# Products in two parts for the experts' units of 128 slots, results added with exact ones, and weights in ten tiles of 1 MB

## The chip, the cores and the metric

The kernel runs on one core of one Trainium2 chip. The time is device microseconds of one execution of the whole program; each number below says whether it is a median of runs or the execution that was profiled. Engines: PE is TensorE (products), PEld its loading of the stationary operand, DVE VectorE, ACT ScalarE, POOL GpSimd; SP issues DMA transfers. A bank is one of the eight accumulators of TensorE, 128 rows by 512 columns of fp32.

## The reference, cut to what matters

The model has two layers over 256 latent and 256 context tokens of width 1024: an attention layer with a dense feed-forward part, then a state-space layer with a gated linear unit and a mixture of experts. The change lies in the last part alone: eight experts with 3584 hidden columns, each token sent to two of them.

```python
def swiglu(t, w1, w3, w2):
    return (jax.nn.silu(t @ w1) * (t @ w3)) @ w2

def moe_ffn(t, w_router, w1, w3, w2):          # t: 256 x 1024
    logits = (t @ w_router).astype(jnp.float32)
    top_val, top_idx = lax.top_k(logits, TOP_K)          # TOP_K = 2
    gates = jax.nn.softmax(top_val, axis=-1)
    combine = jnp.sum(gates[..., None] * (top_idx[..., None] == jnp.arange(N_EXPERTS)), axis=-2)
    out = jnp.zeros_like(t)
    for e in range(N_EXPERTS):
        out = out + combine[..., e:e + 1] * swiglu(t, w1[e], w3[e], w2[e])
    return out
...
    h = layer_norm(DEEPNORM_ALPHA * h + mod[:, :, 5] * f, ln_g[layer, 1], ln_b[layer, 1])
```

All data are fp32, and the result is wanted to fp32 accuracy.

## The kernel before

Everything ahead of the experts is the same in both kernels. It ends with `n`, two tiles of 128 tokens by 1024, and a table of which token goes to which expert.

**Slots and units.** The experts are ranked by their number of tokens. Rank 0 has room for 192 tokens (slots), the others for 128, 96, 96, 64, 32, 32 and 32 (`CAPS`). What does not fit is left to a loop at the end (`overflow`), which runs no time with these inputs. The slots of an expert are worked on in units of 128, 64 or 32 (`KINDS`): rank 0 has one of 128 and one of 64, rank 1 one of 128, ranks 2 and 3 one of 64 and one of 32, rank 4 one of 64, the last three one of 32. `gather` fills the tile `xg` (1024 x 672 slots, turned) by products of `n` with one-hot matrices `G`.

**Chunks.** The 3584 hidden columns are cut in seven chunks of 512, so there are 56 chunks of 6 MB: a third of `w1` (tile `wa`), one of `w3` (`wb`) and one of `w2` (`wc`), 2 MB each. They pass through a ring of seven tiles (`K.mwb = 7`). The bytes are the same whatever the rank, 336 MB in all; the products are not: ranks 0 to 3 are called heavy, 4 to 7 light. `chunk_order` mixes them by a sum of costs (`COST`): it puts a heavy chunk where the products lag behind the loads, and a light one otherwise. The order that comes out, with H for heavy and L for light, is `LLHLLHLHLLHLLHLLHLLHLHLHLLHLHLHLHLHLHHHLHHHHLHHHHHHHLLLL` and takes the heavy ranks as 0, 1, 2, 3.

**A unit.** `unit_hidden` makes two banks (`p1`, `p3`) in fp32. For 128 slots the weights are the stationary operand, 32 products of 128 columns per matrix (L1517), and the result already lies turned. For 64 or 32 slots the tokens are stationary and the products lie side by side in the columns of the engine (L1526). ACT takes the silu (L1531), DVE multiplies (L1532). `unit_turn` turns a narrow unit's result (L1543), `unit_out` multiplies by `wc` (L1555; 8 products of 512 columns for 128 slots) and adds the two halves to the unit's sum `ya` (L1561, L1563). After the seventh chunk the sum is multiplied by the row `g5` (L1565) and added to both token tiles by `combine` (L1575, L1576), a product with the one-hot matrix of the unit's slots times the gates (`combine_matrix`, L1485, L1487).

**Order.** The loop in `moe` runs one unit ahead: products of `wa` for unit i, the turn of unit i-1, products of `wb` for unit i, `unit_out` of unit i-1. The loads of a chunk are issued on SP's queue when its first unit comes up (L1602, L1605, L1608), each waiting for a free tile. `rest` puts between units the spreading of rows of parameters over partitions (L2147, L2150). `n` and these rows stay in tiles (`rn`, `row`). A scheduler sets the order of the other engines' instructions on their queues from the program order and its own estimates.

Of the kernel before, what the change touches and what calls it, by code (L numbers as in the profile page):

```python
# [20 lines left out]
D = 1024  # L21
# [8 lines left out]
NE = 8  # L30
# [1263 lines left out]
NSLOT = sum(CAPS)  # L1294
ORDER = (7, 0, 6, 1, 2, 5, 3, 4)
# [136 lines left out]
def overflow_list(K, pool, R):  # L1432
# [6 lines left out]
    scr = pool.tile([128, D], F32, tag="ya", name="scr", bufs=4)  # L1439
# [26 lines left out]

def onehots(K, pool, R):
    nc = K.nc
    G = []
    for i in range(2):  # L1470
        G.append(pool.tile([128, NSLOT], F32, tag="ya", name="G", bufs=4))
        for r in range(NE):
            nc.vector.tensor_scalar(G[i][:, BASE[r]:BASE[r] + CAPS[r]], R.iota192[:, :CAPS[r]], R.pos[:, i, r:r + 1], None,
                                    op0=ALU.is_equal)
    return G


def combine_matrix(K, pool, R, kind, base, pos, gate, tag, bufs):
# [7 lines left out]
    c = pool.tile([128, 256], F32, tag=tag, name="cmb", bufs=bufs)  # L1486
# [4 lines left out]
def gather(K, n, G, lo, hi, xg, A, B):  # L1491
    nc = K.nc
    N = hi - lo
    for k in range(8):
# [3 lines left out]
        if k % 2:  # L1498
            nc.scalar.activation(xg[:, k, lo:hi], ps[:, :N], AF.Identity, scale=A[:, k, 1:2], bias=B[:, k, 1:2])
        else:  # L1500
            nc.vector.tensor_scalar(xg[:, k, lo:hi], ps[:, :N], A[:, k, 1:2], B[:, k, 1:2], op0=ALU.mult, op1=ALU.add)


def unit_hidden(K, pool, kind, x, w13a, w13b, between=None):
# [5 lines left out]
    if G == 1:  # L1510
        gT = pool.tile([128, 4, 128], F32, tag="mgT", name="mgT", bufs=4)
        for w, p in ((w13a, p1), (w13b, p3)):
            if between and p is p3:
                between()
            for b in range(4):
                for k in range(8):
                    nc.tensor.matmul(p[:, b * 128:(b + 1) * 128], lhsT=w[:, k, b * 128:(b + 1) * 128],  # L1517
                                     rhs=x[:, k, :], start=(k == 0), stop=(k == 7))
        g = gT.rearrange("p b s -> p (b s)")
    else:  # L1520
        for w, p in ((w13a, p1), (w13b, p3)):
            if between and p is p3:
                between()
            for k in range(8):
                for q in range(G):
                    nc.tensor.matmul(p[kind * q:kind * (q + 1), :N], lhsT=x[:, k, :], rhs=w[:, k, q * N:(q + 1) * N],  # L1526
# [3 lines left out]
    sl = pool.tile([128, 512], F32, tag="msl", name="msl", bufs=2)[:, :N]  # L1530
# [5 lines left out]
def unit_turn(K, pool, kind, st):  # L1536
    gT, g = st
    if gT is None:
        nb = 4 * kind // 128
        gT = pool.tile([128, 4, 128], F32, tag="mgT", name="mgT", bufs=4)  # L1540
# [4 lines left out]
    return gT  # L1545


def unit_out(K, kind, gT, w2, ya, first, last):
# [3 lines left out]
    for b in range(nb):  # L1552
        for hf in range(2):
            for q in range(G):
                K.nc.tensor.matmul(Y[hf][kind * q:kind * (q + 1), :], lhsT=gT[:, b, kind * q:kind * (q + 1)],  # L1555
                                   rhs=w2[:, q * nb + b, hf * 512:(hf + 1) * 512],
                                   start=(b == 0), stop=(b == nb - 1))
    for hf in range(2):
        o = slice(hf * 512, (hf + 1) * 512)
        if first:  # L1560
            K.nc.scalar.copy(ya[:, o], Y[hf])  # L1561
        else:
            K.nc.vector.tensor_tensor(ya[:, o], Y[hf], ya[:, o], op=ALU.add)  # L1563
# [48 lines left out]
def moe(K, pool, R, G, n, A, B, rest):  # L1612
# [19 lines left out]
    def out(j):  # L1632
# [8 lines left out]
        if j["ch"] == final:  # L1641
            combine(K, c, ya.pop(key))
# [631 lines left out]
```

## Time and profile before

| | before |
|---|---|
| median of 3 runs | 1824.44 us (1817.72 to 1825.11) |
| the profiled execution | 1823.15 us |
| its span in the trace | 1821.3 us |
| busy share: PE, PEld, DVE, ACT, POOL | 93%, 64%, 46%, 22%, 11% |
| mean DMA rate over the span | 305 GB/s |
| granted clock of PE, mean | 0.971 of full |

The shares are means over the whole span, of which the experts' stage is the second half; a stage of its own can be quite unlike the mean. A product in fp32 counts as two instructions in the trace. The time of the profiled execution is its span and 1.9 us around it.

### The profile page before, as it was taken

How to read it: one execution, taken by the hardware profiler on the slowest of the kernel's cores; microseconds unless marked ns; L12 is line 12 of the kernel's file. 1: busy time of each engine (PE TensorE's matmuls, PEld its weight loads, DVE VectorE, ACT ScalarE, POOL GpSimd, SP SyncE). 2: the span in 40 equal slices, each digit the busy share in tenths (PEclk: the TensorE clock that was granted, in tenths of full speed). 3: DMA queues.
4: the chain of work that ended last, by engine and by line, in shares of the span. 5: the costliest groups of instructions: out<-in, count | busy, mean ns of one | idle time of the engine just before them, and what ended most of it. 6: DMA issues, size and time to landing. Idle time of an engine off the chain costs nothing.

```text
span 1821.3 us, 34632 instructions
## 1 busy us (share of the span) xinstructions
PE 1687.4 (93%) x14673; PEld 1169.2 (64%) x14673; DVE 835.5 (46%) x1480; ACT 409.5 (22%) x775; POOL 206.1 (11%) x295
## 2 busy tenths in 40 slices
PE   6999997999897999658899999999999999999996
PEld 3755576777675777446577767676667665555553
DVE  2755568858978478995612121113011131241244
ACT  2555543222212355433220000000000001001001
POOL 7910005000000000463120000000000000000000
PEclk9999999999998999788899999999999999999998
DMA  8478752368877776876699799998999998999995
GB/s 318 162 240 270 261 192 82 127 217 278 272 249 239 254 250 202 244 196 264 249 427 401 297 411 389 417 426 350 373 427 412 382 396 322 426 425 377 392 392 207
DMA packets 118391, 556.25 MB, mean 305 GB/s; under 512 B 14616, under 2 KB 47068, under 8 KB 93400
## 3 DMA queue, kind: packets, MB, share of 16 engines
q1 hardware_dynamic: 116800, 550.29, 80.1%
q0 software_dynamic: 1248, 3.10, 0.5%
q8 instruction: 118, 1.93, 0.4%
q10 hardware_dynamic: 184, 0.59, 0.1%
q14 instruction: 41, 0.34, 0.1%
HBM read 529.41 MB, written 24.54 MB: 304 GB/s over the span
## 4 chain that ended last, share of the span: by engine, by line
PE 60%; DVE 10%; DMA 8%; issue 2%; SPq 1%; ACT 1%; POOL 0%; DVEq 0%; ACTq 0%; POOLq 0%
PE bank L1526 18%; PE bank L1555 13%; PE bank L1517 11%; PE bank L57 4%; PE bank L59 4%; PE bank L58 3%; DMA w_d<-wt 2%; PE bank L1575 2%; DMA wraw<-in_ffn_w 1%; PE bank L1497 1%; DMA wb<-in_s_bw 1%; DVE whl L52 1%; PE bank L1543 1%; DVE sG L1122 1%; DMA wa<-in_moe_w 1%
## 5 line engine op out<-in xcount | busy, mean ns | idle before, releaser
L1555 PE MATMUL bank<-wc,mgT 128*32 128x512 f32 (+2 forms) x1200 | 266.0, 598 | 0.5 <-DVE mgT L44 0.5
L1531 ACT ACTIVATE msl<-bank 128x128 f32<-128x128 f32 (+2 forms) x77 | 28.8, 374 | 729.1 <-PE bank L1526 555.3
L52 DVE TENSOR_TENSOR whl<-wraw,whl 128x1024 fp32r<-128x1024 f32 (+3 forms) x126 | 151.0, 1201 | 80.0 <-ACT whl L51 79.9
L59 PE MATMUL bank<-u,whl 128*128 128x512 f32 (+1 forms) x416 | 164.9, 396 | 20.1 <-DVE whl L52 20.1
L51 ACT CAST whl<-wraw 128x1024 fp32r<-128x1024 f32 (+3 forms) x126 | 125.7, 998 | 240.3 <-PE bank L59 109.2
L57 PE MATMUL bank<-u,whl 128*128 128x512 f32 (+1 forms) x416 | 167.4, 402 | 3.9 <-DVE u L52 3.9
L1555 PEld LDWEIGHTS bank<-wc,mgT 128*32 128x32 f32 (+2 forms) x1200 | 85.7, 134 | 132.4 <-issue 127.8
L1526 PE MATMUL bank<-wb,xg 128*32 128x128 f32 (+1 forms) x3136 | 170.5, 304 | 0.0
L1526 PE MATMUL bank<-wa,xg 128*32 128x128 f32 (+1 forms) x3136 | 170.1, 304 | 0.0
L1526 PEld LDWEIGHTS bank<-wa,xg 128*32 128x32 f32 (+1 forms) x3136 | 123.7, 118 | 70.5 <-PE bank L1555 18.7
L58 PE MATMUL bank<-u,whl 128*128 128x512 f32 (+1 forms) x416 | 163.8, 394 | 0.0
L1563 DVE TENSOR_TENSOR ya<-bank,ya 128x512 f32<-128x512 f32 x128 | 88.4, 691 | 139.4 <-PE bank L1555 139.2
L1526 PEld LDWEIGHTS bank<-wb,xg 128*32 128x32 f32 (+1 forms) x3136 | 122.3, 117 | 37.5 <-issue 3.7
L1532 DVE TENSOR_TENSOR msg<-msl,bank 128x128 f32<-128x128 f32 (+1 forms) x63 | 21.9, 347 | 267.7 <-PE bank L1526 267.7
L1517 PEld LDWEIGHTS bank<-xg,wa 128*128 128x128 f32 x896 | 104.4, 196 | 9.9 <-PE bank L1555 6.5
L1517 PE MATMUL bank<-xg,wa 128*128 128x128 f32 x896 | 105.9, 280 | 0.5 <-DMA wa<-in_moe_w 0.5
L59 PEld LDWEIGHTS bank<-u,whl 128*128 128x128 f32 x416 | 80.5, 193 | 40.4 <-DVE whl L52 22.6
L1517 PE MATMUL bank<-xg,wb 128*128 128x128 f32 x896 | 102.3, 275 | 0.0
L1746 POOL TENSOR_TENSOR y<-y,row 128x512 f32<-128x512 f32 x2 | 3.0, 1507 | 875.5 <-ACT y L1745 875.5
L1517 PEld LDWEIGHTS bank<-xg,wb 128*128 128x128 f32 x896 | 101.2, 192 | 0.0
L57 PEld LDWEIGHTS bank<-u,whl 128*128 128x128 f32 x416 | 80.6, 194 | 27.8 <-DVE u L52 4.9
L58 PEld LDWEIGHTS bank<-u,whl 128*128 128x128 f32 x416 | 80.7, 194 | 17.8 <-issue 0.8
(504 smaller groups left out, 2410.1 us busy)
## 6 DMA issues: line engine op xcount, KB each, us to landing
wa<-in_moe_w SPq DMA_DIRECT2D x56, 2048.0 KB
wb<-in_moe_w SPq DMA_DIRECT2D x55, 2048.0 KB
wc<-in_moe_w SPq DMA_DIRECT2D x55, 2048.0 KB
wraw<-in_ffn_w SPq DMA_DIRECT2D x88, 512.0 KB
adaw<-in_ada_w SPq DMA_DIRECT2D x80, 512.0 KB
wraw<-in_w_o SPq DMA_DIRECT2D x16, 512.0 KB
wf<-fs_d SPq DMA_DIRECT2D x32, 256.0 KB
wb<-in_s_bw SPq DMA_DIRECT2D x32, 256.0 KB
```

Source lines behind the costliest of these rows:

```text
L51: K.nc.scalar.copy(hi, src)
L52: (eng or K.nc.vector).tensor_tensor(lo, src, hi.bitcast(F32), op=ALU.subtract)
L57: mm(ps, lhsT=l[0], rhs=r[1], start=start, stop=False)
L58: mm(ps, lhsT=l[0], rhs=r[0], start=False, stop=False)
L59: mm(ps, lhsT=l[1], rhs=r[0], start=False, stop=stop)
L1517: nc.tensor.matmul(p[:, b * 128:(b + 1) * 128], lhsT=w[:, k, b * 128:(b + 1) * 128], rhs=x[:, k, :], start=(k == 0), stop=(k == 7))
L1526: nc.tensor.matmul(p[kind * q:kind * (q + 1), :N], lhsT=x[:, k, :], rhs=w[:, k, q * N:(q + 1) * N], start=(k == 0), stop=(k == 7))
L1531: nc.scalar.activation(sl, p1[:, :N], AF.Silu)
L1532: nc.vector.tensor_tensor(g, sl, p3[:, :N], op=ALU.mult)
L1555: K.nc.tensor.matmul(Y[hf][kind * q:kind * (q + 1), :], lhsT=gT[:, b, kind * q:kind * (q + 1)], rhs=w2[:, q * nb + b, hf * 512:(hf + 1) * ...
L1563: K.nc.vector.tensor_tensor(ya[:, o], Y[hf], ya[:, o], op=ALU.add)
L1575: nc.tensor.matmul(ps, lhsT=c[:, i * 128:(i + 1) * 128], rhs=ya[:, o], start=True, stop=True)
```

## The change

A unit of 128 slots now goes by `wide_hidden`, `wide_turn` and `wide_out`: the tokens are stationary, and each operand is split in a part that is rounded to fp32r (ACT) and the rest of it (DVE, `split`); a product is three passes of 512 columns on the parts (`mm3`). `gather` makes the 256 wide slots in two parts at once. The weights are split when they are needed, in pieces of 128x1024, into pairs of tiles from a ring of four: two of its own, one where `n` lay, one where two parameter rows lay. `Parts.more` makes the splits in program order as far as a pair is free.

The sum of a unit is added with ones: the matrix of slots holds exact ones, the gate is multiplied into the sum on DVE together with `g5`, and the sum is split in two parts (`yh`), so that two passes do. The last expert's sum is added as before.

The weights pass in ten tiles of 1 MB. `wa` and `wb` of a chunk are loaded by `load_in`, `wc` by `load_out`; the loads are issued by the chunk before. The order of the chunks is a string; the heavy ranks come as 2, 1, 0, 3, the light ones as 6, 5, 4, 7. `n` is stored to memory for the overflow loop, two rows of parameters are spread after the last wide unit, and of a chunk's units the wide one comes last.

```diff
-def combine(K, c, ya):
+    unit_add(K, Y, ya, first, last)
...
+        if last is True:
+            K.nc.vector.tensor_tensor(ya[:, o], ya[:, o], K.g5[:, o], op=ALU.mult)
+        elif last is not None:
+            K.nc.vector.scalar_tensor_tensor(ya[:, o], ya[:, o], last, K.g5[:, o], op0=ALU.mult, op1=ALU.mult)
...
+def combine(K, c, ya, hf):
...
+    for i in range(2):
+        ps = K.bank()
+        for z, y in enumerate(ya):
+            nc.tensor.matmul(ps, lhsT=c[:, i * 128:(i + 1) * 128], rhs=y, start=(z == 0), stop=(z == len(ya) - 1))
+        nc.vector.tensor_tensor(K.res[i][:, o], ps, K.res[i][:, o], op=ALU.add)
...
+    def more(S):
+        while S.todo and S.free and len(S.todo[0][0]["w"]) > S.todo[0][1]:
+            job, which, i = S.todo.pop(0)
+            src = job["w"][which][i // 2].rearrange("p k f -> p (k f)")[:, i % 2 * 1024:i % 2 * 1024 + 1024]
+            t = S.free.pop(0)
+            hi, lo = (pool.tile([128, 1024], F32R, tag=tag, name="part") for pool, tag in t)
+            split(S.K, hi, lo, src)
+            S.made.append((job, which, i, t, hi, lo))
...
+def wide_hidden(K, pool, P, j, x, between):
...
+        for i in range(4):
+            t, hi, lo = P.take(j, m, i)
+            for kk in range(2):
+                k, o = 2 * i + kk, slice(kk * 512, kk * 512 + 512)
+                mm3(K, p[m], (x[0][:, k], x[1][:, k]), (hi[:, o], lo[:, o]), k == 0, k == 7)
+            P.give(t)
...
+def wide_out(K, P, j, ya, first, last):
...
+            mm3(K, Y[hf], [x[:, b] for x in j["gT"]], (hi[:, o], lo[:, o]), b == 0, b == 3)
...
+ORDER = "LHHLHLHHHLHHHHLLHHHHLHLLHLLHLLHLLHLLLLHLLLHLHHHLHHHHLLLL"
+def chunk_order():
+    x = {k: iter([(r, c) for r in y for c in range(7)]) for k, y in (("H", (2, 1, 0, 3)), ("L", (6, 5, 4, 7)))}
+    return [next(x[k]) for k in ORDER]
...
+        w.append([K.mw.tile([128, 4, 512], F32, tag="mw", name=name, bufs=K.mwb) for _ in range(2)])
...
+                yh = pool.tile([128, 2, 512], F32R, tag="yh", name="yh", bufs=2)
+                split(K, yh[:, 0], yh[:, 1], y[:, o])
+                combine(K, c, [yh[:, x] for x in range(2)], hf)
...
     for i in range(n - 2):
         hidden(jobs[i], (lambda: turn(jobs[i - 1])) if i else None)
         if i:
+            P.more()
             out(jobs[i - 1])
-        rest(i)
+        if jobs[i]["u"] == 0:
+            load(jobs[i]["c"] + 1, True)
+        rest(i, i == done + 1)
+        if i:
+            P.more()
...
-    K.mwb = 7
+    K.mwb = 10
```

Two places of VectorE's queue. First, wide units of rank 1. Before, with a unit of 128 between units of 64 (`mgT` is a wide unit's hidden tile, `msg` a narrow one's, `ya` the sum):

```order
L44 COPY mgT<-bank 128x256
L1532 TENSOR_TENSOR mgT<-msl,bank 128x512
L1563 TENSOR_TENSOR ya<-bank,ya 128x512 x2
L1532 TENSOR_TENSOR msg<-msl,bank 128x256
L1563 TENSOR_TENSOR ya<-bank,ya 128x512 x2
```

After, two wide units of rank 1 in a row; each `part` row is a split of a 128x1024 piece of the tile named, and the row with `mgT<-bank` is the split of the turned tile:

```order
L52 TENSOR_TENSOR mgT<-bank,mgT 128x512
L52 TENSOR_TENSOR part<-wb,part 128x1024 x4
L52 TENSOR_TENSOR part<-wc,part 128x1024 x3
L1658 TENSOR_TENSOR msl<-msl,bank 128x512
L52 TENSOR_TENSOR part<-wc,part 128x1024
L1586 TENSOR_TENSOR ya<-bank,ya 128x512 x2
L52 TENSOR_TENSOR part<-wa,part 128x1024 x4
L52 TENSOR_TENSOR part<-wb,part 128x1024 x2
```

Where one multiplication and two additions stood for a wide unit, the queue now has twelve splits of weights and one of the turned tile as well, and the additions to `ya` of one unit stand ahead of the first four splits for the next one's `wa`, with the split of the turned tile among the splits of weights.

Second, an addition of results. Before (`cmb` is the matrix of slots, `row` holds `g5`, `h_99` and `h_100` are the token tiles):

```order
L1484 TENSOR_SCALAR cmb_t<-rc,pos,gate 128x128 x2
L1563 TENSOR_TENSOR ya<-bank,ya 128x512
L1565 TENSOR_TENSOR ya<-ya,row 128x512
L1563 TENSOR_TENSOR ya<-bank,ya 128x512
L1565 TENSOR_TENSOR ya<-ya,row 128x512
L1576 TENSOR_TENSOR h_99<-bank,h_99 128x512
L1576 TENSOR_TENSOR h_100<-bank,h_100 128x512
```

After (`gcol` is the column of gates, `yh` the split sum, and the token tiles are called `h_100` and `h_101`):

```order
L1586 TENSOR_TENSOR ya<-bank,ya 128x512 x2
L1590 SCALAR_TENSOR_TENSOR ya<-ya,gcol,row 128x512 x2
L52 TENSOR_TENSOR yh<-ya,yh 128x512 x2
L1614 TENSOR_TENSOR h_100<-bank,h_100 128x512
L1614 TENSOR_TENSOR h_101<-bank,h_101 128x512
L1614 TENSOR_TENSOR h_100<-bank,h_100 128x512
L1614 TENSOR_TENSOR h_101<-bank,h_101 128x512
```

Between the additions to `ya` and those to the token tiles there were two multiplications, each behind its own addition; there are now two multiplications and two splits, behind both additions.

## Rows read from the trace of the kernel before

**Rows 1.** Timeline of TensorE, first unit: start us, us, engine, line, operation, out<-in, count

```profile
918.99 1.95 PE L1526 MATMUL bank<-wa,xg 128*32 128x128 f32 x64
...
922.62 3.71 PE L2147 MATMUL bank<-rows,ident 20*128 20x256 f32 x16
```

**Rows 2.** Timeline of TensorE, the last products

```profile
1797.83 1.95 PE L1526 MATMUL bank<-wb,xg 128*32 128x128 f32 x64
...
1805.34 2.36 PE L1711 MATMUL bank<-y,cmb 128*128 128x256 f32 x8
```

**Rows 3.** Stretches: busy us and count by engine, granted clock, DMA share, GB/s

```profile
440.00:480.00 40.00, 32.51 (x245) 24.29 (x245) 31.17 (x41) 8.75 (x16) 0.00 (x0) 0.91 0.78 260
848.00:858.00 10.00, 10.00 (x45) 8.09 (x44) 3.98 (x4) 2.18 (x3) 0.00 (x0) 1.00 1.02 413
1020.00:1060.00 40.00, 40.00 (x317) 30.25 (x319) 4.90 (x9) 3.75 (x8) 0.00 (x0) 0.91 0.68 281
1320.00:1400.00 80.00, 80.00 (x556) 54.97 (x555) 11.78 (x19) 2.61 (x6) 0.00 (x0) 1.00 1.00 419
919.00:1808.00 889.00, 877.33 (x9574) 576.52 (x9573) 193.97 (x369) 59.53 (x143) 9.33 (x4) 1.00 0.94 386
840.00:860.00 20.00, 18.64 (x81) 15.12 (x82) 8.30 (x7) 5.49 (x7) 0.22 (x1) 1.00 0.88 345
```

**Rows 4.** Waits in the stage, of SP and TensorE: us in total, times, longest

```profile
SPq L1602 <- PE bank L1555: 286.5, 21, 22.8
...
PE bank L1517 <- DMA wa<-in_moe_w: 0.5, 1, 0.5
```

**Rows 5.** Timeline of TensorE, units and an addition of results

```profile
1202.76 1.96 PE L1526 MATMUL bank<-wa,xg 128*32 128x128 f32 x64
...
1208.51 7.40 PE L1517 MATMUL bank<-xg,wa 128*128 128x128 f32 x64
1215.75 0.27 PE L1543 MATMUL bank<-ident,msg 128*128 128x128 f32 x1
...
1224.96 3.67 PE L1526 MATMUL bank<-wa,xg 128*64 128x256 f32 x32
...
1232.01 0.44 PE L1485 MATMUL bank<-ident,cmb_t 128*128 128x128 f32 x2
1232.29 7.03 PE L1555 MATMUL bank<-wc,mgT 128*128 128x512 f32 x16
1240.07 3.67 PE L1575 MATMUL bank<-ya,cmb 128*128 128x512 f32 x8 [0.74 <-DVE ya L1565]
1243.67 1.95 PE L1526 MATMUL bank<-wa,xg 128*32 128x128 f32 x64
...
1248.17 3.65 PE L1555 MATMUL bank<-wc,mgT 128*64 128x512 f32 x16
```

**Rows 6.** Timeline of TensorE, second spread and a slow matrix

```profile
949.20 0.69 PE L2147 MATMUL bank<-rows,ident 20*128 20x256 f32 x2
...
954.21 3.67 PE L1526 MATMUL bank<-wa,xg 128*64 128x256 f32 x32
...
1024.13 10.24 PE L1517 MATMUL bank<-xg,wa 128*128 128x128 f32 x64
```

**Rows 7.** Timeline of TensorE, three-pass products ahead of the stage

```profile
862.31 0.39 PE L57 MATMUL bank<-wg,zT 128*128 128x512 f32 x1
...
863.01 0.40 PE L57 MATMUL bank<-wg,zT 128*128 128x512 f32 x1
```

**Rows 8.** Instructions by form on VectorE: count, busy us, mean ns, idle before

```profile
L52 DVE TENSOR_TENSOR whl<-wraw,whl 128x1024 fp32r<-128x1024 f32 x106 | 134.1, 1268 | 62.5 <-ACT whl L51 62.5
L1563 DVE TENSOR_TENSOR ya<-bank,ya 128x512 f32<-128x512 f32 x128 | 88.4, 691 | 139.4 <-PE bank L1555 139.2
```

**Rows 9.** The page, GB/s in 40 slices of the span

```profile
GB/s 318 162 240 270 261 192 82 127 217 278 272 249 239 254 250 202 244 196 264 249 427 401 297 411 389 417 426 350 373 427 412 382 396 322 426 425 377 392 392 207
```

**Rows 10.** Timeline of SP, the first load of an expert weight

```profile
893.92 0.38 SPq L1602 DMA_DIRECT2D wa<-in_moe_w  x1
```

More of the change, by code (lines that the diff above doesn't have):

```diff
@@ L1545, in unit_turn, with unit_add @@
     return gT
+def unit_add(K, Y, ya, first, last):
+    for hf in range(2):
+        o = slice(hf * 512, (hf + 1) * 512)
+        if first:
+            K.nc.scalar.copy(ya[:, o], Y[hf])
+        else:
+            K.nc.vector.tensor_tensor(ya[:, o], Y[hf], ya[:, o], op=ALU.add)
+        if last is True:
+            K.nc.vector.tensor_tensor(ya[:, o], ya[:, o], K.g5[:, o], op=ALU.mult)
+        elif last is not None:
+            K.nc.vector.scalar_tensor_tensor(ya[:, o], ya[:, o], last, K.g5[:, o], op0=ALU.mult, op1=ALU.mult)
 def unit_out(K, kind, gT, w2, ya, first, last):
@@ L1555, in unit_out @@
                 K.nc.tensor.matmul(Y[hf][kind * q:kind * (q + 1), :], lhsT=gT[:, b, kind * q:kind * (q + 1)],
-                                   rhs=w2[:, q * nb + b, hf * 512:(hf + 1) * 512],
+                                   rhs=half(w2, q * nb + b)[:, hf * 512:(hf + 1) * 512],
                                    start=(b == 0), stop=(b == nb - 1))
[L1558 to L1563, printed above, removed]
-        if last:
-            K.nc.vector.tensor_tensor(ya[:, o], ya[:, o], K.g5[:, o], op=ALU.mult)
@@ new lines, in wide_turn @@
+def wide_turn(K, pool, g):
+    pt = K.bank()
+    for b in range(4):
+        K.nc.tensor.transpose(pt[:, b * 128:(b + 1) * 128], g[:, b * 128:(b + 1) * 128], K.ident)
+    gT = [pool.tile([128, 4, 128], F32R, tag="mgT", name="mgT", bufs=5) for _ in range(2)]
+    split(K, *(x.rearrange("p b s -> p (b s)") for x in gT), pt)
+    return gT
+def wide_out(K, P, j, ya, first, last):
+    Y = K.bank(), K.bank()
+    for b in range(4):
+        t, hi, lo = P.take(j, 2, b)
+        for hf in range(2):
+            o = slice(hf * 512, hf * 512 + 512)
+            mm3(K, Y[hf], [x[:, b] for x in j["gT"]], (hi[:, o], lo[:, o]), b == 0, b == 3)
+        P.give(t)
+    unit_add(K, Y, ya, first, last)
@@ L1619, in moe, with load @@
     jobs = []
+    P = Parts(K, ring + [[(pool, "ph%d" % i), (pool, "pl%d" % i)] for i in range(2)])
+    def load(c, third):
+        if c == len(order):
+            return
+        r, ch = order[c]
+        if r not in e:
+            e[r] = nc.sync.value_load(R.eid[0:1, r:r + 1], min_val=0, max_val=NE - 1)
+        if third:
+            load_out(K, W[c], e[r], ch, c == len(order) - 1)
+        else:
+            load_in(K, W[c], e[r], ch)
     def hidden(j, between=None):
         if j["u"] == 0:
-            r = j["r"]
```

216 lines of the change are left out of this document (138 added, 78 removed).

## The prediction

> **What bounds the kernel now.** I read the page first: by the shares in the table above PE is the fullest engine. The change touches only the experts' stage, so I took that stretch alone, from the first product of an expert unit at 918.99 to the last product, 1805.34 + 2.36 = 1807.70, which is 888.7 us [rows 1, 2]. Over 919 to 1808 PE is busy 877.3 of 889.0 us, and the DMA share is 0.94 [rows 3]: two resources are nearly full at once. The waits say which one ends last. PE waited for weights once, 0.5 us, while SP, which issues the loads, waited on PE for a free weight tile 286.5 us in one of its rows alone [rows 4]. So PE bounds the stage, and the transfers are ahead by as much as the room allows; they cannot be far from being the bound themselves.
>
> I checked that reading with the time of each unit on PE, taken as start to start in the timeline. A unit of 32 slots takes 1202.76 to 1208.51, 5.8 us. One of 64 takes 7.05 for its first two matrices (1224.96 to 1232.01), 3.65 for the last and 0.44 for turning (two transposes, as the row at 1232.01 has them), 11.1. One of 128 takes two matrices of 7.24 (1208.51 to 1215.75) and one of 7.03, 21.5. An addition of results (transposes 0.28, from 1232.01 to 1232.29; wait 0.74; products 3.60, from 1240.07 to 1243.67) takes 4.6 [rows 5]. Of the three spreads of rows the first takes 3.7 and the second 5.0, and I count the third like the first [rows 1, 6]. By ranks: rank 0, 7 x 32.6; rank 1, 7 x 21.5; ranks 2 and 3, 14 x 16.9; rank 4, 7 x 11.1; the last three, 21 x 5.8; 11 additions, 50.6; spreads 12.4: 878 in all, and with 8 for the end 886 against 888.7 traced. Of the rest, 2.9 is one matrix at a lower clock (10.24 us against 7.40) [rows 5, 6].
>
> **The change, part by part.**
> *Wide units.* 64 + 8 fp32 products become 24 x 3 products of 512 columns on parts. The kernel already has such products: three of them take 0.70 us start to start, 0.233 each [rows 7]. 72 x 0.233 + 0.6 for four transposes = 17.4 us, so each of 14 units saves 4.1 and all save 57. Unmeasured here is only whether the splits keep pace. A split of 128x1024 takes 1.27 on DVE, and its rounding runs on ACT meanwhile; twelve make 15.2 us of DVE per unit, and four other DVE steps of 0.69 bring it to 18.0 [rows 8], a little over PE's 17.4. Between narrow units that is covered, since four parts may be made ahead. Where two wide units follow each other (rank 1: twice and three times) the order shows the two additions to ya ahead of the next unit's splits: 0.69 + 1.27 and some 0.2 of handing over (an estimate) make 2.2 us in which PE has no part, and the split of the turned tile stands between two splits of wb. I take 2.2 for each of 5 such places. Below that it could be 0, if the scheduler's other order (splits first) holds; above, 4, if both waits add up.
>
> *Additions of results.* Four products (3.60) become eight on parts (1.87), in ten of eleven cases. But the chain ahead of them grows: after PE's last product come one addition, two multiplications and one subtraction on DVE, 4 x 0.69, and about 0.2 of handing over: 3.0 us instead of the traced 0.74 [rows 5, 8]. PE has nothing else queued there. So an addition costs 0.28 + 3.0 + 1.87 = 5.2 instead of 4.6: ten of them lose 6. Bounds: the chain could stay at 0.7 (a gain of 17) or, where splits of parts stand ahead of it on DVE, reach 5 (a loss of 26).
>
> *PE alone* would then end 57 - 6 - 11 = 40 us earlier.
>
> *Weights.* The bytes stay. A transfer now has rows of 8 KB per partition instead of 16. At the latter, 1320 to 1400 moved 419 GB/s; the only full stretch with rows of 8 and 4 KB, 848 to 858, 413 [rows 3]. For a 1 MB tile that is 2.50 to 2.54; I take 2.5, 15.0 us per chunk of six, from the nearer row; the other end of the bound is the 427 GB/s of the best slice of the page, 2.46 and 14.7 [rows 9]. 56 chunks at 15.0 are 840 us. The first load is issued at 893.92 [rows 10], 25 us before the first unit, so *transfers alone* would end 919 - 25 + 840 = 1734: 74 us early too.
>
> *Room.* This is where I think the gain goes. Before, seven tiles of 2 MB (14 MB); after, ten of 1 MB. PE works on the first two thirds of chunk c+1 before the last third of chunk c, so six of the ten tiles are bound and four, 10 us of transfers, are the most that can lie ahead (before: three of seven bound, four tiles of 2 MB, 20 us). With a lead of only 10 us, PE's surplus in one stretch no longer pays for the transfers of the next. Each stretch of the order takes the longer of its two sums, and a stretch bound by transfers gets back 10 us once.
>
> Heavy ranks come 2, 1, 0, 3, light ones 6, 5, 4, 7. Rank 0 takes 28.5 now, rank 1 17.4.
> - Chunks 1 to 14 (four light, seven of rank 2, three of rank 1; PE): 23.2 + 118.3 + 34.8 + 11.8 (the last without its output) + spreads 8.7 + two additions 10.4 + two back-to-back waits 4.4 = 211.6.
> - LL (transfers): 30 - 10 = 20.
> - HHHH of rank 1, L, first of rank 0 (PE): 69.6 + 6.6 + 5.8 + 28.5 + 10.4 = 120.9.
> - LLHLLHLLHLL, eleven chunks (transfers): 165 - 10 = 155; PE needs about 143 and gets no help from it.
> - H LLLL H LLL H: three of rank 0 on PE, 85.5, and light runs by transfers, 60 - 10 and 45 - 10: 170.5.
> - L HHH L HHHH (PE): 11.6 + 118.3 + three additions 15.6 + a spread 3.7 = 149.2.
> - LLLL (transfers): 60 - 10 = 50; and the end as traced from 1799.78 (1797.83 + 1.95) to 1807.70 [rows 2], 7.9.
>
> Together 885.1 us, 3.6 less than the 888.7 traced. *Hidden at no cost:* the wide gather (the same 672 columns), the store of n (POOL, 1 MB under the first units), one-hots in other places. The rest of the program stays.
>
> *Clock.* The new waits have a second price. The one stretch of the stage with a lower mean clock, 1020 to 1060, has 0.91, and a matrix in it took 2.9 us longer; in 440 to 480, where PE was busy 32.5 of 40 us, the clock was 0.91 too, while the busy 1320 to 1400 have 1.00 [rows 3, 6]. The Trainium skill, TensorE: Matmul & The Clock Gate, Part 1, says that the half clock is the default and that idleness brings it back: it speaks against a change that gives PE waits. The trace agrees in direction. I put nothing into the sum, since most waits fall where transfers are the bound, and keep the price as a rival.
>
> **The rivals.**
> *No change (0.39).* The sum: 1823.15 - 3.6 = 1819.5 for the profiled execution; the median shown lies 1.3 higher, so I say **1821**. Less than 0.5% (9 us) is about what a measurement of this kernel cannot tell from nothing.
> *Faster (0.33).* The waits at additions and between wide units are filled by the scheduler, in the stretches bound by PE alone: seven additions x 2.3 and five waits x 2.2 make 27 us; and transfers run at 14.7 in the 24 chunks that they bound, 7 us. 1821 - 34 = 1787. For it: DVE's mean share in the stage is only 22% (194 of 889) [rows 3]. Against: the chain is serial and PE's queue holds nothing in between. It decides from 6 us of these 34 on. A gain of all 40 would need the room not to matter, which I hold for unlikely.
> *Slower by the clock (0.16).* Six PE-bound pieces start right after a wait; if two matrices in each run at the longer time, 12 x 2.9 = 35 us: 1856; with one, 1838. It decides from five such matrices on. For it: the 10.24 us row. Against: PE still has work some nine tenths of the time.
> *Slower by the transfers (0.12).* If a 1 MB tile takes 2.68 us, as where 345 GB/s came at a share of 0.88 (392 GB/s at full share, 840 to 860) [rows 3], a chunk takes 16.1, and 24 chunks cost 26 us: 1847. It decides from 15.6 us per chunk on (12 us). Against: the full stretch at 413.
>
> The chances by sign come from these: faster 0.33, no change 0.39, slower 0.28. The likeliest case's own range is 1812 to 1830; for 8 in 10 I reach to 1787 and to 1850.
>
> **What would show it.** In the profile after: products of a wide unit start every 0.23 us and a unit's sum is near 17.4; PE busy in the stage falls to about 835, with waits on DMA, in light runs, of some 40 to 50 us in all where there was 0.5; SP still waits for tiles in the heavy runs; 3 us before the products of an addition; about 2 us between wide units of rank 1; a 1 MB tile every 2.5 us when the queue is full. I would be wrong if PE's waits on weights are under 15 us (then the room does not matter and the time is near 1780), if wide units take 20 us throughout because splits limit them (then over 1850), or if the clock in the stage falls below 0.95.

## The result, and the profile after

The changed kernel takes 1849.52 us (median of 4 runs, 1841.94 to 1852.65), the kernel before 1824.78 beside it: a ratio of 1.0143, 95% interval 1.0102 to 1.0183. It is 1.4% slower. The time lies at the upper edge of the range, and the forecast of no change was wrong.

The head of the page after:

```profile
span 1844.6 us, 34002 instructions
...
PE 1666.0 (90%) x13721; PEld 1139.9 (62%) x13721; DVE 1061.3 (58%) x1706; ACT 601.9 (33%) x981; POOL 206.8 (11%) x297
```

PE is busy 21 us less than before and the span is 23 us longer: what was saved in products became idle time. VectorE and ScalarE have the splits, 226 and 192 us more than the page of before had (835.5 and 409.5).

The same stage, from the first product of a unit at 914.64 to the last at 1830.38, 915.7 us against 888.7, and the seven stretches of the prediction, as windows (columns as in [rows 3]):

```profile
914.60:1830.40 915.80, 855.65 (x8622) 546.59 (x8621) 410.85 (x561) 249.43 (x345) 9.30 (x4) 0.97 0.93 375
914.60:1151.40 236.80, 217.57 (x2426) 137.98 (x2429) 88.20 (x126) 59.31 (x87) 9.30 (x4) 0.94 0.91 364
1151.40:1171.30 19.90, 15.85 (x302) 12.21 (x302) 8.75 (x14) 4.18 (x6) 0.00 (x0) 1.00 1.00 403
1171.30:1292.00 120.70, 112.33 (x616) 81.67 (x616) 96.17 (x107) 67.68 (x76) 0.00 (x0) 0.94 0.89 357
1292.00:1451.10 159.10, 149.83 (x1595) 98.31 (x1593) 74.72 (x94) 51.06 (x68) 0.00 (x0) 0.99 1.01 416
1451.10:1621.90 170.80, 165.41 (x1122) 102.37 (x1121) 79.09 (x102) 47.87 (x63) 0.00 (x0) 1.00 0.97 395
1621.90:1779.00 157.10, 150.04 (x1929) 89.46 (x1929) 41.06 (x78) 15.16 (x37) 0.00 (x0) 0.98 0.86 343
1779.00:1830.40 51.40, 44.62 (x648) 24.58 (x647) 22.86 (x45) 4.17 (x9) 0.00 (x0) 0.97 0.90 365
```

Of the stage PE was busy 855.7 us and idle 60.2; before it was 877.3 and 11.4 [rows 3]. The clock fell from 1.00 to 0.97. By stretch:

| chunks | forecast us | measured us | PE idle us | clock |
|---|---|---|---|---|
| 1 to 14 | 211.6 | 236.8 | 19.2 | 0.94 |
| 15, 16 | 20 | 19.9 | 4.1 | 1.00 |
| 17 to 22 | 120.9 | 120.7 | 8.4 | 0.94 |
| 23 to 33 | 155 | 159.1 | 9.3 | 0.99 |
| 34 to 43 | 170.5 | 170.8 | 5.4 | 1.00 |
| 44 to 52 | 149.2 | 157.1 | 7.1 | 0.98 |
| 53 to 56 | 57.9 | 51.4 | 6.8 | 0.97 |

The stretches called bound by transfers came out within some 4 us, the last one 6.5 shorter. Four fifths of the miss of 30.6 us (915.7 against 885.1) lie in the first one, 25.2 us, which was called bound by PE. That chunks 17 to 22 came out right to 0.2 us is luck in part: PE was idle 4 us less there than the sum has it, and busy 4 us more.

PE's waits after, the longest first (us in total, times, longest):

```profile
PE bank L1613 <- ACT yh L51: 24.0, 11, 4.1
PE bank L1558 <- DMA wa<-in_moe_w: 20.2, 11, 3.2
PE bank L57 <- DVE part L52: 8.4, 5, 4.1
PE bank L1613 <- DVE ya L1588: 2.1, 1, 2.1
PE bank L1613 <- DVE yh L52: 2.1, 1, 2.1
...
PE bank L1558 <- DMA wb<-in_moe_w: 0.5, 2, 0.3
```

That is 28.2 us at additions, 20.7 for weights and 8.4 for splits; before there were 8.1 us at additions and 0.5 us for weights [rows 4]. The waits on weights are short and many, eleven of the thirteen on `wa`, of at most 3.2 us. The first three long ones stand in chunks 1 to 14, each at a heavy chunk that follows a single light one. PE there:

```profile
971.40 3.68 PE L1558 MATMUL bank<-wa,xg 128*64 128x256 f32 x16 [3.16 <-DMA wa<-in_moe_w]
...
978.16 1.89 PE L1558 MATMUL bank<-wb,xg 128*64 128x256 f32 x16
979.99 1.90 PE L1600 MATMUL bank<-wc,mgT 128*32 128x512 f32 x10
981.82 1.95 PE L1558 MATMUL bank<-wb,xg 128*64 128x256 f32 x16
983.70 0.63 PE L1600 MATMUL bank<-wc,mgT 128*32 128x512 f32 x3
983.72 0.62 PE L1558 MATMUL bank<-wa,xg 128*32 128x128 f32 x4
984.15 0.60 PE L1600 MATMUL bank<-wc,mgT 128*32 128x512 f32 x3
984.58 1.92 PE L1558 MATMUL bank<-wa,xg 128*32 128x128 f32 x60
...
1001.18 5.36 PE L1558 MATMUL bank<-wa,xg 128*64 128x256 f32 x32 [3.09 <-DMA wa<-in_moe_w]
```

Three things are to be read here. The matrix at 1001.18 has waited 3.09 us for its weights and then takes 5.36 us; the same 32 products took 3.67 at 945.52 (below). The one at 971.40 took 3.68 for its first half after 3.16 of waiting, where half a matrix takes 1.89 (978.16). And the products do not stand as they did in [rows 5]: the 16 instructions (eight products) of `wc` for a unit of 32 are cut in 10, 3 and 3, with products of `wb` and of the next unit between. Whole they take some 1.8 us (1.75 from 952.98 to the next start, in the same trace); here 1.83 (979.99 to 981.82) and, from 983.70 to 984.58, another 0.88 with four cheap instructions between.

SP in the same stretch, the issues of the weight loads:

```profile
954.93 0.91 SPq L1699 DMA_DIRECT2D wb<-in_moe_w  x2
956.08 1.09 SPq L1708 DMA_DIRECT2D wc<-in_moe_w  x2
958.09 1.21 SPq L1699 DMA_DIRECT2D wa<-in_moe_w  x2
963.56 1.21 SPq L1699 DMA_DIRECT2D wb<-in_moe_w  x2
965.71 1.21 SPq L1708 DMA_DIRECT2D wc<-in_moe_w  x2
968.26 0.96 SPq L1699 DMA_DIRECT2D wa<-in_moe_w  x2
984.77 0.91 SPq L1699 DMA_DIRECT2D wb<-in_moe_w  x2
```

Twelve tiles are issued within 14 us (954.93 to 968.26), then none for 15.5. Tiles come free in bursts, when the second unit of a chunk passes.

### The profile page after: what moved, and what is told of

Its sections match the earlier page's. It is cut to its first block, busy times and chain, and to the rows that moved or that the text cites. A ratio compares the mean times of both kernels' runs of the same rounds, so it can differ in the third digit from the quotient of the medians.

```text
span 1844.6 us, 34002 instructions
## 1 busy us (share of the span) xinstructions
PE 1666.0 (90%) x13721; PEld 1139.9 (62%) x13721; DVE 1061.3 (58%) x1706; ACT 601.9 (33%) x981; POOL 206.8 (11%) x297
## 3 DMA queue, kind: packets, MB, share of 16 engines
q0 software_dynamic: 1536, 4.15, 0.7%
## 4 chain that ended last, share of the span: by engine, by line
PE 66%; DMA 14%; DVE 12%; issue 3%; ACT 2%; SPq 1%; POOL 1%; DVEq 0%; ACTq 0%; POOLq 0%
PE bank L1558 16%; PE bank L57 12%; PE bank L59 11%; PE bank L58 11%; PE bank L1600 7%; DMA wa<-in_moe_w 5%; DMA wb<-in_s_bw 2%; PE bank L121 2%; DMA w_d<-wt 2%; DMA adaw<-in_ada_w 2%; PE bank L1613 2%; DMA wb<-in_moe_w 1%; DVE whl L52 1%; PE bank L1518 1%; DMA wraw<-in_ffn_w 1%
## 5 line engine op out<-in xcount | busy, mean ns | idle before, releaser
L1558 PE MATMUL bank<-wa,xg 128*32 128x128 f32 (+1 forms) x3136 | 194.3, 317 | 20.2 <-DMA wa<-in_moe_w 20.2
L1600 PE MATMUL bank<-wc,mgT 128*32 128x512 f32 (+1 forms) x976 | 189.0, 598 | 0.2 <-DVE mgT L44 0.2
L1558 PEld LDWEIGHTS bank<-wa,xg 128*32 128x32 f32 (+1 forms) x3136 | 135.8, 122 | 84.7 <-issue 41.4
L1558 PE MATMUL bank<-wb,xg 128*32 128x128 f32 (+1 forms) x3136 | 180.8, 305 | 0.8 <-DMA wb<-in_moe_w 0.5
L1558 PEld LDWEIGHTS bank<-wb,xg 128*32 128x32 f32 (+1 forms) x3136 | 123.7, 117 | 55.2 <-issue 26.1
L1563 ACT ACTIVATE msl<-bank 128x128 f32<-128x128 f32 (+1 forms) x63 | 20.5, 325 | 353.2 <-PE bank L1558 353.1
L1600 PEld LDWEIGHTS bank<-wc,mgT 128*32 128x32 f32 (+1 forms) x976 | 50.4, 121 | 85.7 <-issue 79.6
L57 PE MATMUL bank<-part,xw 128*128 128x512 f32 x224 | 93.2, 416 | 8.4 <-DVE part L52 8.4
L58 PE MATMUL bank<-part,xw 128*128 128x512 f32 x224 | 90.2, 403 | 0.0
L59 PE MATMUL bank<-part,xw 128*128 128x512 f32 x224 | 90.2, 403 | 0.0
L52 DVE TENSOR_TENSOR part<-wb,part 128x1024 fp32r<-128x1024 f32 x56 | 68.1, 1224 | 27.4 <-ACT part L51 26.4
```

The costliest lines, as they stand in the source:

```text
L52: (eng or K.nc.vector).tensor_tensor(lo, src, hi.bitcast(F32), op=ALU.subtract)
L57: mm(ps, lhsT=l[0], rhs=r[1], start=start, stop=False)
L58: mm(ps, lhsT=l[0], rhs=r[0], start=False, stop=False)
L59: mm(ps, lhsT=l[1], rhs=r[0], start=False, stop=stop)
L1563: nc.scalar.activation(sl, p1[:, :N], AF.Silu)
```

## The experiments

Times are medians of 4 to 10 runs, beside the kernel before on the same chip (1820 to 1825 us). The time ahead of the stage varied by up to 17 us between executions (the first product of a unit came between 909.7 and 926.5), so I compare stages too: the table holds, from the row of the stage in the one profiled execution of each run, its length, PE's busy and idle time and the clock.

| run | median us | ratio to before, interval | stage | PE busy | PE idle | clock |
|---|---|---|---|---|---|---|
| before | 1824.78 | | 888.7 | 877.3 | 11.4 | 1.00 |
| changed kernel | 1849.52 | 1.0143 (1.0102 to 1.0183) | 915.8 | 855.7 | 60.2 | 0.97 |
| e1, TensorE as written | 1844.02 | 1.0122 (1.0091 to 1.0153) | 910.3 | 843.2 | 67.1 | 0.96 |
| e2, additions of before | 1853.27 | 1.0158 (1.0117 to 1.0198) | 914.5 | 862.0 | 52.5 | 0.98 |
| e3, half the bytes | 1782.80 | 0.9791 (0.9762 to 0.9819) | 846.6 | 817.3 | 29.3 | 0.99 |
| e4, wide units of before | 1893.13 | 1.0384 (1.0347 to 1.0420) | 960.0 | 910.2 | 49.8 | 0.97 |
| e5, half the bytes, five tiles | 1791.13 | 0.9804 (0.9776 to 0.9833) | 856.6 | 822.7 | 33.9 | 0.98 |
| e6, order of before | 1840.10 | 1.0085 (1.0066 to 1.0104) | 905.8 | 855.4 | 50.4 | 0.98 |
| e7, before with five tiles | 1879.19 | 1.0303 (1.0285 to 1.0321) | 949.0 | 891.9 | 57.1 | 0.97 |
| e8, eleven tiles | 1858.19 | 1.0178 (1.0134 to 1.0222) | 919.2 | 859.8 | 59.4 | 0.96 |
| e9, late additions, as written | 1810.39 | 0.9938 (0.9917 to 0.9959) | 880.4 | 828.7 | 51.7 | 0.98 |
| e10, e9 in the order of before | 1804.07 | 0.9909 (0.9877 to 0.9940) | 866.1 | 826.8 | 39.3 | 0.98 |
| e11, e9 in another order | 1800.34 | 0.9887 (0.9851 to 0.9923) | 866.1 | 824.0 | 42.1 | 0.98 |
| e12, late additions, scheduler | 1827.95 | 1.0032 (1.0012 to 1.0052) | 891.9 | 848.1 | 43.8 | 0.98 |
| e13, e11 with eleven tiles | 1787.31 | 0.9807 (0.9767 to 0.9847) | 856.2 | 825.9 | 30.3 | 0.98 |
| e14, before, late additions, as written | 1810.53 | 0.9941 (0.9917 to 0.9964) | 878.6 | 875.2 | 3.4 | 1.00 |

**e1_pe_as_written.**

```diff
-        lastly = moe(K, mw, R, G, n, ...)
+        with tc.manual_schedule(engines={ENG.PE}):
+            lastly = moe(K, mw, R, G, n, ...)
```

> TensorE runs the loop over units in the order in which it is written; nothing else is changed against the changed kernel (1849.5 us). First theory: a third of the loss is that the scheduler cut the products of narrow units in pieces and laid them between one another (a block of 16 products of wc in pieces of 10, 3 and 3, of 8 or 16 of wa and wb between them). Start to start the narrow products cost 543.8 us in the trace of after against 506.3 before, and some 16 of these 37.5 are pieces, not a lower clock. As written they should cost about 528, the waits on weights stay near 21 us or grow by a few, and the time comes near 1835 (1829 to 1842). Rival: the pieces only fill time in which TensorE would wait for a weight anyway; then the time stays within 4 us of 1849.5 and the waits on weights grow by what the products lose.

Between the two: 1844, with an interval that overlaps the changed kernel's. In the stage PE's busy time fell by 12.5 us, so the pieces do cost, but its idle time rose by 6.9: waits on weights from 20.7 to 26.1, at additions from 28.2 to 30.2.

**e2_additions_before.**

```diff
-        whole = j["r"] == jobs[-1]["r"]
-        final = 4 if whole else 6
+        whole = True
+        final = 4 if j["r"] == jobs[-1]["r"] else 6
```

> The ten additions of results are made as in the kernel before (gates in the matrix, sum not split, four fp32 products); the rest is the changed kernel. First theory: in after TensorE waited 28 us for the chain on VectorE ahead of the additions, against 8 before, and its products there became only 8 us cheaper, so undoing it gives 12 us back, and a little more if the half clock after these waits goes: 1836 (1830 to 1841). Rival: the waits at additions let the transfers run ahead, and what is won here is lost in the next light run: 1845 to 1851, with the waits on weights up from 21 us to 30 or more.

No gain: 1853. The rival's time, but not by its reason alone: the waits on weights rose by only 2.5 us (23.2 from 20.7). Even with the shorter chain the additions waited 18.2 us, not 8; at the two longest (3.1 and 2.9 us) two splits of weights stand ahead of or within the chain on VectorE. Their products took 9 us more again.

**e3_half_the_bytes.**

```diff
-        w.append([K.mw.tile([128, 4, 512], ...) for _ in range(2)])
-        for i in range(2):
+        w.append([K.mw.tile([128, 4, 512], ...)] * 2)
+        for i in range(1):
```

(and the same for `wc`)

> Only the first tile of each pair of 1 MB weight tiles is loaded, and the products read it for both halves, so half of the expert weights is left out; the products, splits and additions are all made. Transfers can then not be late. In this kernel the scheduler also leaves the products of narrow units whole, so it stands beside the run with TensorE's order as written. First theory: the waits on weights (21 us) go, the half clock right behind them (about 13 us, eight matrices that took 1.5 to 1.8 us longer) goes too, and the pieces (16 us): 1800 (1793 to 1808), with waits at additions (28 us) and at splits (8 us) as in after, and half clock left only behind these. Rival: the clock falls whatever the waits on weights, by the products on parts or the additions; then only 21 + 16 us go, 1813 or more, and a dozen stretches of half clock remain.

1782.8, 17 us below the forecast: a larger gain than the range allowed. Its stage as a window:

```profile
919.30:1765.90 846.60, 817.27 (x8622) 526.56 (x8621) 409.69 (x561) 251.50 (x345) 9.32 (x4) 0.99 0.56 198
```

69 us less than after. No wait on a weight and none on a split is left (8.4 after). The additions still wait 26 us. Against e1, in which the narrow products are whole too, PE is busy 26 us less for the same products, at a mean clock of 0.99 against 0.96: that is the half clock.

**e4_wide_units_before.**

```diff
-            j["g"] = wide_hidden(K, pool, P, j, [x[:, :, lo:lo + 128] for x in xw], between)
+            j["gT"], j["g"] = unit_hidden(K, pool, 128, xw[:, :, lo:lo + 128], ...)
```

(and no splits, turns or `wide_out`)

> The units of 128 slots are made in fp32 as in the kernel before, with no splits; order of chunks, ten tiles of 1 MB, additions and loads are those of the changed kernel. First theory: products on parts save 52 us start to start (303.1 before, 251.2 after), of which 13 are given back by waits on splits (8.4) and the half clock behind them (4.6). Undone, the time rises by 39, less what the transfers gain by the slower products: 1885 (1876 to 1890). Rival: the splits (170 us of ScalarE and 200 of VectorE) slow the rest, additions and turns of narrow units, as much as the products gain; then it stays near 1850 to 1865.

1893, 44 more than the changed kernel and 3 above the range: the products on parts are worth 8 us more than this run's forecast had them, and the loss is elsewhere.

**e5_half_bytes_same_room.**

```diff
-    K.mwb = 10
+    K.mwb = 5
```

(on e3)

> Half of the expert weights is left out, as in the run at half the bytes (1782.8 us), but the ring has five tiles instead of ten, so that it holds as many thirds of a chunk as the changed kernel's; each third is one transfer of 1 MB and not two. Theory of the room: a chunk in hand binds eight of ten tiles until its last unit begins (third of w2 of the chunk before, all three of its own), so only two lie ahead when it ends, and six transfers of 2.5 us must then land within some 13 us. With half the bytes these six thirds take 7.5 us, within the 13, so the waits stay few: 1785 to 1800, with under 6 us of waits on weights. Rival: it is not the time of the transfers but the late release and the way from issue to landing; then most of the waits come back, and the time is above 1815.

1791, as the theory of the room says, with no wait on weights. The room of the changed kernel costs no such wait when the transfers take half the time, so the loss needs both: few tiles and the full time of the transfers. The stage is still 10 us longer than in e3; 5 of these are PE's busy time.

**e6_order_before.**

```diff
-ORDER = "LHHLHLHHHLHHHHLLHHHHLHLLHLLHLLHLLHLLLLHLLLHLHHHLHHHHLLLL"
+ORDER = "LLHLLHLHLLHLLHLLHLLHLHLHLLHLHLHLHLHLHHHLHHHHLHHHHHHHLLLL"
...
-    ... ("H", (2, 1, 0, 3)) ...
+    ... ("H", (0, 1, 2, 3)) ...
```

> The changed kernel with the order of chunks of the kernel before (string and heavy ranks 0, 1, 2, 3); the rest as changed. Theory of the room: single light chunks between heavy ones are what the ring of ten can't feed, and in the order of before ranks 0 and 1, whose wide units let go of their tiles as the splits go on, stand where the light ones are; worked out with the unit times of the trace, 2.5 us a tile and ten tiles, the stage comes out some 20 us shorter than with the changed order: 1829 (1818 to 1840), waits on weights down from 21 to about 12. Rival: the changed order is the one that suits the ring; then the time rises, to 1860 or more, and waits on weights with it.

1840.1: waits on weights 11.9, as said, the time half way to the 1829 that was said. The order costs some 10 us with ten tiles, no more.

**e7_before_five_tiles.** `K.mwb = 5` in the kernel before.

> The kernel before with five tiles of 2 MB instead of seven: the room of the changed kernel, and nothing else of it. Theory of the room: fp32 products everywhere, the order of before and whole tiles, and yet the same loss: waits on weights from 0.5 to over 40 us, half clock behind them, 1880 to 1915. Rival: the loss belongs to the changed order and to the loads by halves, and before needs only five tiles: 1820 to 1835.

1879, 55 us slower than before and 1 us below the range, with nothing of the change but the room. PE's waits:

```profile
PE bank L1517 <- DMA wa<-in_moe_w: 34.8, 6, 6.8
PE bank L1575 <- DVE ya L1565: 8.1, 11, 0.9
PE bank L1526 <- DMA wa<-in_moe_w: 5.1, 1, 5.1
PE bank L1526 <- DMA wb<-in_moe_w: 4.6, 5, 1.3
PE bank L1692 <- DMA wc<-in_moe_w: 2.7, 2, 2.1
```

47 us of waits on weights where there was 0.5, and the clock at 0.97 where it was 1.00; PE is busy 14.6 us longer for the same products. The loss is of the changed kernel's kind, though its waits are fewer and longer (up to 6.8 us).

**e8_eleven_tiles.**

```diff
-    K.mwb = 10
+    K.mwb = 11
...
-                    yh = pool.tile([128, 2, 512], F32R, tag="yh", name="yh", bufs=2)
+                    yh = pool.tile([128, 2, 512], F32R, tag="yh", name="yh", bufs=1)
```

(and msl 3 to 2, mgT 5 to 4)

> The changed kernel with eleven tiles of 1 MB. The space comes from one buffer less of yh (two to one), of msl (three to two) and of mgT (five to four). Theory of the room: half of a chunk's lead more, so a single light chunk between heavy ones finds its successor's wa there: waits on weights and splits fall from 29 us by about a half, with the clock behind them: 1834 (1826 to 1842). Rival: the transfers are simply too slow for this order (more room is filled once and then empty again), or the buffers taken away cost as much: 1845 to 1855.

Missed: 1858. The waits on weights and splits fell from 29.1 to 21.4 us, but with one `yh` buffer those at additions rose from 28.2 to 34.9. The run could not decide; e13 does.

**e9_late_additions, e10_order_before_late, e11_other_order.** The products of an addition go behind the next unit's products with `wa`; TensorE as written.

```diff
-                    combine(K, c, [yh[:, x] for x in range(2)], hf)
+                    late.append((c, [yh[:, x] for x in range(2)], hf))
...
     def turn(j):
         j["gT"] = wide_turn(K, pool, j["g"]) if ... else unit_turn(...)
+        while late:
+            combine(K, *late.pop(0))
```

e10 has e6's order as well, e11 heavy ranks 0, 2, 1, 3 and `LLHLLHLHLLHLLHLHLLHLLLHHHLHHLLHHLLHHLHHLHHHLHHHLHHHHLLLL`.

> The changed kernel with TensorE's order as written and the products of an addition moved behind the next unit's products with wa, so that the chain on VectorE ahead of them (one addition, two multiplications, one subtraction per half) lies beside products. Two theories on what the 26 us of waits at additions are worth. If TensorE's waits simply add up: 1844 (the run as written) less some 26 and the half clock behind them, 1815. If the ring of ten is the bound, as the run with the additions of before suggests (12 us expected there, none measured), the transfers take part of it: waits at additions gone, waits on weights up from 26 us to 32 or more, 1828 to 1838. I hold the second for likelier.

> The same two edits on the changed kernel with the order of chunks of before (1840.1 us without them). There the waits on weights are 12 us and those on splits 10, so less of what is won at the additions goes into them. If the ring is the bound only where single light chunks stand between heavy ones, the 24 us of waits at additions and some 10 us of pieces and half clock come out of the time: 1810 (1802 to 1820), which is faster than the kernel before. If the ring takes it here too: 1825 or more.

> The same two edits and an order of chunks worked out for ten tiles from the unit times of the trace, 2.5 us a tile and the release of each tile: heavy ranks 0, 2, 1, 3, and after a beginning as in the kernel before two or three heavy and two light chunks in turn. It comes out 21 us shorter than the order of before in that reckoning, with waits on weights under 10 us. If the reckoning of the room is right: 1795 (1785 to 1808). If the ring of ten has costs that it leaves out (such as tiles freed in bursts), 1810 to 1825.

1810, 1804 and 1800, all faster than before. In e9 I held the wrong one for likelier. PE's waits there:

```profile
PE bank L1558 <- DMA wa<-in_moe_w: 28.7, 14, 4.7
PE bank L57 <- DVE part L52: 11.4, 8, 4.9
PE bank L1558 <- DMA wb<-in_moe_w: 4.0, 8, 0.9
PE bank L1842 <- DMA wc<-in_moe_w: 2.7, 2, 2.4
PE bank L1613 <- DVE yh L52: 1.1, 3, 0.5
```

The waits at additions are gone (2 us, from 30.2 in e1), those on weights and splits rose from 33.9 in e1 to 46.8, so nearly half was taken back; PE's idle time fell by 15.4. PE's busy time fell by 14.5 more; 10 of these are the products of the additions (31.6 us start to start in e1, 21.2 in e9). e11's order gave little of what I had worked out for it: it was to be 21 us shorter than the order of before, and against e10 the median is 3.7 us shorter, the stage equal (866.1) and the waits on weights 23.9 us instead of under 10. What that reckoning leaves out is not shown.

**e12_late_scheduler.** The late additions without TensorE's order as written.

> The changed kernel with the additions of results late, and TensorE's order left to the scheduler, which still cuts narrow products in pieces. If the waits at additions by themselves are the loss (26 us, and 7 us of products at half clock behind them): 1818 (1811 to 1826). If the pieces matter as much once the additions don't wait: 1828 to 1838, halfway between the changed kernel and the run with both edits.

1828, so of the 39 us between the changed kernel and e9 21.6 come with the late additions and 17.6 more with TensorE's order as written. Taken the other way round, the order gave 5.5 (e1) and the late additions then 33.6: the two are worth more together than one by one. In the stage PE is busy 19.4 us less in e9 than here, with the same products.

**e13_eleven_tiles_late.** e11 with e8's buffers; the second half of an addition goes behind the products with `wb`.

> The run with the other order (1800.3 us) with eleven tiles; space from one yh, msl and mgT buffer each, and the second half of an addition placed behind the products with wb, so that one yh does. It still waits 21 us for weights and 14 for splits. If the room is what is left: 11 us less of waits and some half clock, 1787 (1778 to 1794). If the buffers given up cost as much, or the transfers are simply the bound: 1797 to 1806.

1787.3, as the theory of the room says. PE's waits and the stage as a window:

```profile
PE bank L57 <- DVE part L52: 13.5, 7, 3.0
PE bank L1558 <- DMA wa<-in_moe_w: 7.7, 7, 2.1
PE bank L1558 <- DMA wb<-in_moe_w: 4.0, 8, 0.8
PE bank L1844 <- DMA wc<-in_moe_w: 1.2, 2, 0.7
```

```profile
916.30:1772.50 856.20, 825.90 (x8622) 531.00 (x8621) 406.82 (x561) 248.92 (x345) 9.33 (x4) 0.98 0.98 401
```

On weights PE now waits 12.9 us in all, against 23.9 in e11. The waits on splits stayed (13.5 and 13.9). It is 2% faster than before, the lowest time here of a kernel with the whole computation. Beside the tile and the buffers the place of the second halves of the additions changed; the waits at additions are under 2 us in both runs, so the gain is not there.

**e14_before_late.** The two edits of e9 in the kernel before.

> The kernel before with late additions and TensorE's order as written. It waits 8.1 us at its eleven additions, its products are fp32 and whole already. If late additions only take their own wait away: 1813 (1809 to 1818), and the changed kernel with the same edits (1810) has then caught up with it and no more. If it gains nothing (the transfers are as near in this kernel, DMA share 0.94): 1818 to 1823.

1810.5, within its range and the time of e9. With additions late in both, the change as it stands gains nothing and loses nothing.

## Why the prediction was wrong

*What bounds the kernel, and PE alone.* Right, with some luck. Without transfers in the way the stage is 846.6 us (e3), 42 less than before; the prediction had 40. Two misses cancel in it: the waits between wide units (11 forecast) are gone, and the products of ten additions take 29 us start to start instead of 19.

*Wide units.* Right in size: by e4, 44 us in the whole; at full clock, in e3, the 1008 products of the wide units take 237 us start to start, 0.235 each. The waits for splits (11 forecast, 8.4 traced) have two causes. The longest, 4.07 us at 1171.32, stands behind two light chunks, and ScalarE's rounding there waited for `wa` (4.74 us). Two of 2.06 and 1.92 us stand between wide units of rank 1 and are the chain that was forecast at 2.2: ahead of 1226.35, ScalarE had begun on the pieces of `wa` at 1220.33, and VectorE made the two additions to `ya` from 1223.79 and its first split from 1225.08. That is two places of the five; at another, splits stand first. In e3 all are gone: between the wide units there VectorE has splits of `wa` (1172.63) ahead of the additions (1175.02), the other order that the prediction names for a wait of 0.

*Additions.* The wait was right, 2.6 us each (26.1 for ten) against 3.0. The products were not: 28.3 us start to start for the ten, 2.8 each instead of 1.87; in e9 they take 2.1. Behind some of the waits they run at half clock, and at the two in chunks 1 to 14 splits of weights stand ahead of or within the chain on VectorE. One addition on PE, and VectorE ahead of it:

```profile
1107.51 1.92 PE L1600 MATMUL bank<-wc,mgT 128*32 128x512 f32 x16
1113.59 3.80 PE L1613 MATMUL bank<-yh,cmb 128*128 128x512 f32 x8 [4.15 <-ACT yh L51]
```

```profile
1108.34 2.35 DVE L52 TENSOR_TENSOR part<-wa,part 128x1024 fp32r<-128x1024 f32 x2
1110.61 0.42 DVE L1505 TENSOR_SCALAR cmb<-bank 128x256 fp32r<-128x256 f32 x1
1110.94 1.28 DVE L1586 TENSOR_TENSOR ya<-bank,ya 128x512 f32<-128x512 f32 x2
1112.14 1.40 DVE L1590 SCALAR_TENSOR_TENSOR ya<-ya,gcol,row 128x512 f32<-128x512 f32 x2
...
1113.72 1.28 DVE L52 TENSOR_TENSOR yh<-ya,yh 128x512 fp32r<-128x512 f32 x2
```

PE's products of `wc` end at 1109.43. VectorE first makes two splits (`part`) and the matrix of slots (`cmb`), then two additions and two multiplications; ScalarE's rounding of the first half of the sum ends PE's wait of 4.15 us, and VectorE's part of that split comes after. The eight products then took 3.80 us, at a granted clock of 0.55.

*Room: the step that failed.* Of PE's 40 us the transfers were to take back 36; they took 69 (e3 against after). The reckoning was: six of ten tiles are bound, four lie ahead, and a stretch takes the longer of its two sums, with the clock priced at zero and the narrow units at their old times. But `wc` of a chunk is loaded ahead of the next chunk's `wa`, and a chunk of two units frees nothing until its second unit passes. Until the last unit of chunk 3 comes up (the issues at 954.93), the ring holds `wc` of chunk 2, all of chunk 3, and of chunk 4 only `wa`, issued at 936.18: eight bound, two ahead. Six transfers then stand up to `wa` of chunk 5, which PE was ready for at 968.24, 13.3 us later; at 2.5 us they take 15 and some for the way, and PE starts at 971.40. So one light chunk between two heavy ones is enough for a wait, inside a stretch whose sums say that PE is the bound; that happened three times in chunks 1 to 14. e7 shows that the room does this without any other part of the change, e13 that one tile more nearly halves the waits on weights (12.9 us, 23.9 in e11). Of the 25.2 us of the first stretch 9.4 are these three waits, and 16 are products that took longer (PE is busy 217.6 us there, where the sum comes to 201 without its waits). The 69 us are made of:
- 31 us of idle time: 29 of waits on weights and splits, less than the 36 us forecast (40 to 50 us by the list of signs), and 2 at additions;
- 38 us of PE's busy time, from after to e3, which the sum has at nothing. By e1 12.5 of these are the pieces and the other 26, e1 against e3, half clock; e12 against e9 puts 19 on the pieces, which leaves 19 for the clock.

So the miss of 30.6 us lies less in the length of the waits than in what came with them: they are short and many, and stand where PE was to be the bound. The pieces I had not looked for: the narrow units were taken over at their old times (5.8, 11.1), while in the changed kernel's order of TensorE's queue they are cut. In e3, as in the kernel before, they are whole; why the scheduler cuts them in the changed kernel no run shows.

*Transfers.* They were not slower than assumed: 416 GB/s at a full share in chunks 23 to 33, 2.5 us a tile. The rival with 2.68 us did not come about.

*Clock.* Priced at zero, with 1838 to 1856 as a rival at 0.16. The time lies in the rival's range, but the clock is only part of it, 19 to 26 us, and at more places than its six. The Trainium skill, TensorE: Matmul & The Clock Gate, Part 1, was cited for the half clock that idleness brings back. The trace bears it out in direction: in the 3 us behind each of the three waits of 3.1 us in chunks 1 to 14 the granted clock was 0.50 to 0.60, and two of the matrices there took 5.36 us for 3.67, the one at 971.40 took 3.68 and 2.91 for its halves. Not every wait had that price. Of the 21 waits over 1.3 us in the stage, 13 were followed by 3 us at 0.50 to 0.64 and eight by 3 us at 1.00, one of 2.96 us among these (at 1399.17); what tells them apart is not shown.

*What would show it.* PE busy near 835: 855.7. Waits on weights of 40 to 50 in light runs: 20.7, spread over heavy stretches too. 3 us before additions: 2.6. About 2 us between wide units of rank 1: at two places of five. The clock of the stage below 0.95 as a sign of being wrong: 0.97, so it did not show; the two stretches that begin with rank 2 and rank 1 have 0.94.

What stays open: why TensorE's order as written gains 5.5 us alone (e1) and 17.6 once the additions are late; e1's trace shows idle time up by 6.9 us, spread over both kinds of waits.

## What to carry to other kernels

Room in a ring is not tiles times transfer time: list, at the moment when a burst of tiles comes free, which ones are held and which transfer is needed next, and by when. A saving on the bounding engine is worth little while short waits stand in it, since many of them also slow the products behind them; move such waits beside other work first (here late additions gave 21.6 us in the changed kernel, and the kernel before gained 12.5 by the same edits). And read the new order of the engines that were not meant to change.

## What the runs showed of the hardware

The clock also fell where PE had not waited. Behind the spread of rows, 16 instructions (eight products) with 20 of 128 rows, the next matrix ran slowly, and the one of the same shape later did not:

```profile
918.27 3.71 PE L2301 MATMUL bank<-rows,ident 20*128 20x256 f32 x16
921.91 5.36 PE L1558 MATMUL bank<-wa,xg 128*64 128x256 f32 x32
...
945.52 3.67 PE L1558 MATMUL bank<-wa,xg 128*64 128x256 f32 x32
```

The row at 921.91 takes 5.36 us, at a granted clock of 0.68, for the work that takes 3.67 at 945.52, at 1.00. Before, the 10.24 us of [rows 6] came behind such a spread too (third spread, 4.12 us at 1020.09); but behind the first spread there (922.62) the next two matrices took their usual 1.95 us, and only the products of `wc` at 930.18 took 2.64 for 1.90. What brings the clock down there no run shows.

And a block of narrow products that run beside one another loses when it is cut: 16 instructions whole in some 1.8 us, 10, 3 and 3 in some 2.6; the first ten took as long alone as all sixteen. The Trainium skill, TensorE: Matmul & The Clock Gate, Part 3, says that products on different parts of the array run at the same time. The trace agrees: 16 instructions of 512 columns take some 1.8 us in four groups of 32 columns of the engine, and 7.03 where each takes all its columns [rows 5].
